# A two-layer recurrent decoder step: another rank for the token forms, other buffers for the modulation rows, one modulation vector computed earlier

## The chip, the cores and the metric

The kernel runs on one core of a Trainium2 chip. The metric is the device time of one execution in microseconds; the smaller the better.

## What is computed

Two layers over 512 prompt tokens and 8 sample rows of width 1024 (all float32). Cut to what matters here:

```python
mod = einsum('bd,de->be', silu(c), w_ada[l]) + b_ada[l]        # six vectors of 1024 per layer
sh_m, sc_m, gt_m, sh_f, sc_f, gt_f = split(mod, 6)
h = x * (1 + sc_m) + sh_m
out = mixer(h)        # layer 0: GLA and RG-LRU, layer 1: S5 and HGRN2; projections in and out
x = layer_norm(ALPHA * x + (1 + gt_m) * out, ...)
h = x * (1 + sc_f) + sh_f
x = layer_norm(ALPHA * x + (1 + gt_f) * swiglu(h, w_in, w_out), ...)   # hidden width 2816
```

Beside x, the states of the four recurrences are outputs.

## The kernel before

Columns of x are tokens: 2 halves (hf) of 256 prompt tokens and 4 samples each, 260 wide, and 8 blocks (k) of 128 features. The program runs through layer 0's mixer, the first feed-forward, layer 1's mixer (called the odd one) and the second feed-forward; a feed-forward has two parts (hb) of 11 blocks of its hidden width each. Each float32 product is made of three TensorE matmuls on parts "hi" and "lo" of both factors: `mm3` (L284, L286, L288) for a block of both halves, and its one-half form (L865 to L867) for the first units behind a LayerNorm, which start on the first half while the second half is still being normalized.

Weights come through one place, the class WS. SP loads a piece of up to 1 MB (L213) into one of three buffers named raw; ScalarE casts it to whi (L242), VectorE subtracts to get wlo (L111 is the line of every VectorE add, subtract and multiply), and TensorE reads these. The list `plan` gives the order of the pieces; `mix(main, ada)` spreads the pieces "ada" of the modulation weights among the others. One modulation vector is four ada pieces of 1 MB. Each gives 8 matmuls straight from raw (`ada_part`, L372); after the fourth, `ada_rows` copies the row out of PSUM (adasb, L377), transposes it twice (L148), and VectorE adds it into mod. The first two vectors are made at the start, column block by column block, by `ada_mm` (L361, copy L364, L366), each block just ahead of the columns of h that need it. The copies adasb lie in the pool tag t2k, six buffers that many steps share. `layer_norm` makes its columns in a ring of four buffers named h32h (L808 to L816): GpSimd or ScalarE writes h32h, ScalarE the hi part, VectorE subtracts for the lo part (L816).

A scheduler sets the order of the instructions of every engine: it goes by the order of the program, less the offset that `tc.high_priority` gives (a larger offset means earlier; HIGH is 3000). WS prepares weights at offset HIGH. SP's loads run in the order in which it issues them, and it stands when a buffer is not free.

In the odd layer, the S5 input u is turned round through DRAM: four stores Ud and one Usd (L1829, L1849), then ten loads of u (L1851 to L1853), then the matmuls at L1870. In the second feed-forward, eight products per block are replaced by seven in the manner of Strassen (`sw_unit`, L941 to L943); `t_forms` makes the sums and differences of token halves for it (t1, t2, t4, each with hi and lo part), on VectorE and ScalarE.

The change touches lines 329 to 335 (plan), 358 to 364, 375 to 377, 504 and 1020.

Of the kernel before, what the change touches and what calls it, by code (L numbers as in the profile page):

```python
# [7 lines left out]
F32 = mybir.dt.float32  # L8
# [11 lines left out]
HP = 256  # L20
# [13 lines left out]
HIGH = 3000  # L34
# [6 lines left out]
def build(tc, I, O):  # L41
    nc = tc.nc
    V, S, G, T, SY = nc.vector, nc.scalar, nc.gpsimd, nc.tensor, nc.sync
    with ExitStack() as ctx:
        def pool(n, b=1, **k):
            return ctx.enter_context(tc.tile_pool(name=n, bufs=b, **k))

        cst = pool("cst")
# [3 lines left out]
        tmp = pool("tmp", 6)  # L52
# [14 lines left out]
        def mx():  # L67
            return ps["M"].tile([128, 512], F32, tag="mx", name="mx")
# [41 lines left out]
        def tt(out, a, b, op):  # L110
            V.tensor_tensor(out=out, in0=a, in1=b, op=op)  # L111
# [38 lines left out]
        plan = []  # L150
# [144 lines left out]
        def p_ada(l, js):  # L295
            return [("ada", I["w_ada"][l], k0, 2, D * j, D, l) for j in js for k0 in range(0, 8, 2)]
# [19 lines left out]
        def mix(main, ada, first=1, per=2):  # L316
            r = list(main[:first])
            rest = main[first:]
            done = 0
            for n, c in enumerate(rest):  # L320
                want = (n + 1) * (len(ada) // per) // len(rest) * per
                r += ada[done:want]
                done = want
                r.append(c)
            return r

        FA = p_ada(0, [5]) + p_ada(1, [0])
        FB = p_ada(1, [1, 2])
        OA = p_ada(1, [3, 4, 5])
        plan.append(("lr", ev_in, 0, 8, 1536, 16))  # L330
        plan += p_cols("in", ev_in, [0])
        plan += mix(p_cols("in", ev_in, EV_COLS), p_ada(0, range(2, 4)))
        plan += mix(p_cols("out", ev_out, (0, 256)), p_ada(0, [4])[:2], 1) + p_ada(0, [4])[2:] + p_cols("out", ev_out, (512, 768))
        plan += mix(p_ffn(0, 0)[:12], FA[:4], 3) + mix(p_ffn(0, 0)[12:], FA[4:])
        plan += mix(p_ffn(0, 1)[:-4], FB, 2) + p_ffn(0, 1)[-4:]
        plan += mix(p_cols("in", od_in, OD_COLS), OA, 0, 1)
        plan.append(("glu", I["od_s5_w_glu"][0], 0, 4, 0, 512))
        plan += p_cols("out", od_out, range(0, D, 256))
# [16 lines left out]
        def vb(nm, j=0, n=1):  # L355
            return vB[:, vB_off[nm] + j:vB_off[nm] + j + n]

        def ada_mm(p, r):
            for k in range(8):
                c = k % 4  # L360
                T.matmul(p[32 * c:32 * c + 32, 0:256], condT[:, k, :], r[:, k, :],  # L361
                         start=(k < 4), stop=(k >= 4), tile_position=(0, 32 * c), skip_group_check=True)
            sb = tmp.tile([128, 256], F32, tag="t2k", name="adasb")
            S.copy(sb, p[:, 0:256])  # L364
            for b in range(2):
                T.matmul(p[:, 256 + 16 * b:256 + 16 * b + 9], sb[:, 128 * b:128 * b + 128], sel, start=True, stop=True)  # L366
            return p[:, 256:288].rearrange("p (c r) -> p c r", r=16)[:, :, 0:9]
# [5 lines left out]
                             start=(k0 + k == 0), stop=(k0 + k == 7), tile_position=(0, 32 * c), skip_group_check=True)  # L373

        def ada_rows(p, l, j):
            sb = tmp.tile([128, 256], F32, tag="t2k", name="adasb")
            S.copy(sb, p[:, 0:256])  # L377
            for b in range(2):
                transpose(p[:, 256 + 128 * b:384 + 128 * b], sb[:, 128 * b:128 * b + 128])
            tt(mod[l][:, j:j + 8, :].rearrange("p (c b) r -> p b c r", b=2),  # L380
               p[:, 256:512].rearrange("p (b c r) -> p b c r", b=2, r=32)[:, :, :, 0:9],
               bc(vA[:, 48 * l + j:48 * l + j + 8].rearrange("p (c b) -> p b c", b=2).unsqueeze(3), [128, 2, 4, 9]), ALU.add)
# [40 lines left out]
        with tc.tile_pool(name="st", bufs=1, reuse_waits="tile") as st:  # L423
# [73 lines left out]
            for f in range(8):  # L497
                px = mx()
                for q in range(4):
                    transpose(px[:, q * 128:(q + 1) * 128], xin[:, q, f * 128:(f + 1) * 128])  # L500
                S.copy(x[:, f, :, 0:HP], hv(px))
                r = raw0.pop(f)
                with tc.high_priority(offset=2 * HIGH):
                    q = ada_mm(mx(), r)
                if f + 3 < 8:
                    load0(f + 3)
                    if f in (0, 2):
                        loadx(f // 2 + 2)
                if f == 4:
                    ws.load(3)  # L510
                with tc.high_priority(offset=2 * HIGH):
                    tt(mod[0].rearrange("p (c k) r -> p c k r", k=8)[:, 0:2, f, :], q,
                       bc(vA[:, 0:48].rearrange("p (c k) -> p c k", k=8)[:, 0:2, f].unsqueeze(2), [128, 2, 9]), ALU.add)
                    ts1(sc1[:, f], mod[0][:, 8 + f, :], 1.0, ALU.add)
                    h32s.append(modulate(f, sc1, mod[0][:, 0:8, :]))
                act(x[:, f], x[:, f], AF.Copy, scale=ALPHA)
                tc.add_manual_dep(last["act"].ins, last["split"].ins.name, NOSYNC, reason="split first")
                for k in lag[f]:
                    for hf in range(2):
                        T.matmul(lrp[rows[hf], :HN], wl[:, k, :], h32s[k][:, hf], start=(k == 0),  # L520
                                 stop=(k == 7), tile_position=(0, 32 * hf), skip_group_check=True)
# [362 lines left out]
        def ffn(l, mid=None):  # L884
            with tc.tile_pool(name=f"ff{l}", bufs=1, reuse_waits="tile") as fp:
# [92 lines left out]
                for hb in range(2):  # L978
                    f0 = 11 * hb
                    fins = []  # L980
                    for d in range(0, 11, 2):
                        if l and f0 + d >= SW0:
                            break
                        nj = min(2, 11 - d)
                        fins += [(0, d, j) for j in range(nj)] + [(1, d, j) for j in range(nj)]
                    sg = {}

                    def fin_w(up, d, j):
                        return ws.get("fin", DFF * up + 128 * (f0 + d), 0, j)

                    def fin_ev(up, d, j, acc, hs=BOTH):
                        m = d + j
                        if up == 0:
                            if hs.start == 0:
                                sg[m] = t2k("sg")
                            act(sg[m][:, hs], acc, AF.Silu)
                            if hb == 0 and hs.stop == 2 and 3 <= m <= 10:
                                affine(last["act"], [m - 3])
                        else:
                            s_ = sg[m][:, hs]  # L1000
                            mul(s_, acc, s_)
                            split(ah[:, m, hs], al[:, m, hs], s_)
                            if hs.stop == 2:
                                sg.pop(m)

                    n0 = 0
                    if hb == 0:
                        n0 = 5
                        first_units([(lambda u=u: fin_w(*u), lambda acc, hs, u=u: fin_ev(*u, acc, hs)) for u in fins[:n0]], walloc)
                    for u in fins[n0:]:  # L1010
                        w = fin_w(*u)
                        acc = acc_tile()
                        mm3(acc, w, h, range(8))
                        fin_ev(*u, acc[:, :, :HN])
                        if hb == 0 and mid is not None:
                            side = side or mid(fp)
                            next(side, None)
                    if l:
                        if hb == 0:
                            with tc.high_priority(offset=200):  # L1020
                                tf[:] = t_forms()
                        pg.close()
                        with tc.tile_pool(name=f"pS{hb}", bufs=8, space=PSUM, reuse_waits="tile") as ps["S"]:
                            for f in range(max(SW0, f0), f0 + 11):
                                sw_unit(f)
                        pg.enter_context(psum(2, 4, f"g{hb}"))
                        if hb:
                            swx.close()
                    for _ in side or ():
                        pass  # L1030
                    if hb == 0:
                        gt1 = gate1(l, 5)
                    for mp in range(4 - 2 * hb):
                        accs = [acc_tile() for _ in range(2)]
                        for n, (k0, nk) in enumerate(((8, 3), (0, 8))):
                            for j in range(2):
                                w = ws.get("fout", 256 * mp, f0 + k0, j)
                                mm3(accs[j], w, a, range(k0, k0 + nk), n == 0, n == 1, koff=k0)
                        for j in range(2):
                            m = 2 * mp + j  # L1040
                            if hb == 0:
                                evac_a(m, accs[j], gt1)
                            else:
                                evac_y(m, accs[j], gt1)
# [1128 lines left out]
```

## Time and profile before

| | |
|---|---|
| time, median of 3 runs | 1405.61 us (1401.35 to 1406.16) |
| the profiled execution | 1406.39 us, span 1404.6 us, mean granted clock 0.973 |
| PE (TensorE matmuls) busy | 1321.8 us, 94% of the span, 12503 instructions |
| DVE (VectorE) busy | 865.9 us, 62% |
| ACT (ScalarE) busy | 549.4 us, 39% |
| POOL (GpSimd) busy | 187.8 us, 13% |
| moved by DMA | 185.53 MB, 132 GB/s over the span |

The first table of a kernel like this says which engine has no slack; where that engine is busy 94% of the span, the next view to read is the list of its gaps, with what ended each. The mean over the span hides that they lie at few places: the start, the recurrences, and the seams between the stages.

### The profile page before, as it was taken

Reading aid. Unit: us, or ns where it says so; the run is one execution under the profiler, and the core shown is the slowest. Engines: PE = TensorE matmul, PEld = TensorE weight load, DVE = VectorE, ACT = ScalarE, POOL = GpSimd, SP = SyncE. Lnnn points to the kernel's source line nnn. Section 1 sums busy time; section 2 is a strip of 40 time slices with the busy share of each in tenths; the row PEclk is TensorE's granted clock in tenths of the full one; section 3 lists DMA queues with packets and bytes.
Section 4 is the critical chain, followed back from the end, with each engine's and each line's share of the span. In section 5 each row is a group of like instructions: output and inputs, shape, how many; then the busy total and the mean of one; then the engine's idle time right before and its main releaser. Section 6 shows DMA issues by size and latency. Waiting matters only on the chain.

```text
span 1404.6 us, 29570 instructions
## 1 busy us (share of the span) xinstructions
PE 1321.8 (94%) x12503; PEld 1251.7 (89%) x12503; DVE 865.9 (62%) x1946; ACT 549.4 (39%) x962; POOL 187.8 (13%) x215
## 2 busy tenths in 40 slices
PE   6898999999999999999988989999897999999996
PEld 4697987989998999999978889888897999999996
DVE  4677654687998233233682586476937843788565
ACT  3554635353333222222354123344534532455431
POOL 2200010250011200000160251112600000000013
PEclk9998999999999999999999999999999999999998
DMA  9642264413346752445368636632131323332311
GB/s 270 201 149 100 73 199 148 134 48 111 131 162 216 206 174 91 150 132 180 125 226 139 213 120 198 189 110 91 61 91 30 102 84 114 105 93 73 125 61 62
DMA packets 172191, 185.53 MB, mean 132 GB/s; under 512 B 18413, under 2 KB 151915, under 8 KB 171803
## 3 DMA queue, kind: packets, MB, share of 16 engines
q1 hardware_dynamic: 166074, 166.43, 37.9%
q0 software_dynamic: 5744, 17.08, 3.7%
q8 instruction: 98, 1.61, 0.5%
q14 instruction: 35, 0.28, 0.1%
q10 hardware_dynamic: 240, 0.13, 0.0%
HBM read 167.11 MB, written 15.36 MB: 130 GB/s over the span
## 4 chain that ended last, share of the span: by engine, by line
PE 75%; DVE 10%; DMA 7%; issue 3%; ACT 2%; POOL 1%; SPq 1%; POOLq 0%; ACTq 0%; DVEq 0%
PE acc L286 15%; PE acc L284 15%; PE acc L288 15%; PE sb L941 4%; PE sb L943 3%; PE sb L942 3%; PE acc L865 3%; PE acc L867 3%; PE acc L866 3%; PE mx L372 2%; DVE wlo L111 2%; PE mx L148 2%; DMA raw<-in_w_ada_dram 2%; DVE x L111 1%; DMA raw<-in_ffn_w_out_dram 1%
## 5 line engine op out<-in xcount | busy, mean ns | idle before, releaser
L111 DVE TENSOR_TENSOR wlo<-raw,whi 128x1024 fp32r<-128x1024 f32 (+2 forms) x214 | 215.2, 1015 | 182.9 <-ACT whi L242 163.9
L242 ACT CAST whi<-raw 128x1024 fp32r<-128x1024 f32 (+2 forms) x166 | 154.2, 935 | 397.1 <-PE acc L286 269.7
L284 PE MATMUL acc<-hhi,whi 128*128 128x260 f32 x1424 | 294.4, 288 | 3.2 <-ACT hhi L79 0.9
L286 PE MATMUL acc<-hlo,whi 128*128 128x260 f32 x1424 | 293.9, 287 | 0.6 <-DVE hlo L111 0.6
L288 PE MATMUL acc<-hhi,wlo 128*128 128x260 f32 x1424 | 290.9, 286 | 0.0
L284 PEld LDWEIGHTS acc<-hhi,whi 128*128 128x128 f32 x1424 | 220.6, 190 | 15.0 <-issue 5.9
L286 PEld LDWEIGHTS acc<-hlo,whi 128*128 128x128 f32 x1424 | 221.1, 189 | 4.7 <-issue 2.7
L288 PEld LDWEIGHTS acc<-hhi,wlo 128*128 128x128 f32 x1424 | 221.2, 189 | 2.4 <-issue 1.9
L284 PE MATMUL acc<-ah,whi 128*128 128x260 f32 x576 | 117.0, 285 | 3.6 <-ACT whi L242 2.8
L286 PE MATMUL acc<-al,whi 128*128 128x260 f32 x576 | 116.1, 283 | 0.9 <-DVE al L111 0.9
L288 PE MATMUL acc<-ah,wlo 128*128 128x260 f32 x576 | 115.3, 283 | 0.0
L284 PEld LDWEIGHTS acc<-ah,whi 128*128 128x128 f32 x576 | 88.4, 188 | 7.3 <-ACT whi L242 4.3
L286 PEld LDWEIGHTS acc<-al,whi 128*128 128x128 f32 x576 | 88.6, 188 | 1.3 <-DVE al L111 1.3
L288 PEld LDWEIGHTS acc<-ah,wlo 128*128 128x128 f32 x576 | 88.5, 188 | 0.0
L111 DVE TENSOR_TENSOR smp<-acc,gt 128x8 f32<-128x8 f32 (+1 forms) x72 | 11.6, 161 | 110.9 <-PE acc L288 85.7
L865 PE MATMUL acc<-hhi,whi 128*128 128x260 f32 x208 | 60.7, 293 | 3.0 <-ACT hhi L823 2.2
L867 PE MATMUL acc<-hlo,whi 128*128 128x260 f32 x208 | 59.9, 295 | 2.0 <-DVE hlo L111 1.6
L866 PE MATMUL acc<-hhi,wlo 128*128 128x260 f32 x208 | 60.1, 291 | 0.0
L111 DVE TENSOR_TENSOR wxl<-raw,wxh 128x512 fp32r<-128x512 f32 (+1 forms) x74 | 56.3, 777 | 5.0 <-ACT wxh L160 2.9
L111 DVE TENSOR_TENSOR sg<-acc,sg 128x520 f32<-128x520 f32 (+1 forms) x32 | 19.8, 630 | 52.1 <-PE acc L288 47.6
L160 ACT CAST wxh<-raw 128x512 fp32r<-128x512 f32 x64 | 38.3, 619 | 29.0 <-PE sb L942 20.2
L372 PE MATMUL mx<-raw,condT 128*32 128x256 f32 x640 | 45.2, 391 | 2.8 <-DMA raw<-in_w_ada_dram 2.8
(640 smaller groups left out, 2856.5 us busy)
## 6 DMA issues: line engine op xcount, KB each, us to landing
raw<-in_w_ada_dram SPq DMA_DIRECT2D x40, 1024.0 KB, 6.8
raw<-in_ffn_w_in_dram SPq DMA_DIRECT2D x26, 1024.0 KB, 5.1
raw<-in_ffn_w_in_dram SPq DMA_DIRECT2D x36, 512.0 KB, 4.8
raw<-in_ffn_w_out_dram SPq DMA_DIRECT2D x16, 1024.0 KB, 5.2
raw<-in_ev_w_in_dram SPq DMA_DIRECT2D x10, 1024.0 KB, 8.3
raw<-in_od_w_in_dram SPq DMA_DIRECT2D x10, 1024.0 KB, 6.5
raw<-in_w_ada_dram SPq DMA_DIRECT2D x16, 512.0 KB, 7.5
raw<-in_ffn_w_out_dram SPq DMA_DIRECT2D x16, 384.0 KB, 3.0
```

The costliest lines, as they stand in the source:

```text
L111: V.tensor_tensor(out=out, in0=a, in1=b, op=op)
L242: S.copy(hi[:, :nk, :m], rj)
L284: T.matmul(acc[:, hf, :HN], wh[:, k - koff, :], ah(k)[:, hf, :], start=st, stop=False)
L286: T.matmul(acc[:, hf, :HN], wh[:, k - koff, :], al(k)[:, hf, :], start=False, stop=False)
L288: T.matmul(acc[:, hf, :HN], wl[:, k - koff, :], ah(k)[:, hf, :], start=False, stop=sp)
L372: T.matmul(p[32 * c:32 * c + 32, 0:256], condT[:, k0 + k, :], r[:, k, 256 * c:256 * c + 256], start=(k0 + k == 0), stop=(k0 + k == 7), til ...
L865: T.matmul(out, wh[:, k, :], ah(k)[:, hf, :], start=n == 0, stop=False)
L866: T.matmul(out, wl[:, k, :], ah(k)[:, hf, :], start=False, stop=False)
L867: T.matmul(out, wh[:, k, :], al(k)[:, hf, :], start=False, stop=n == len(ks) - 1)
L941: T.matmul(out[:, 0], w[0][:, off + k], t[0][:, k], start=st and k == 0, stop=False, skip_group_check=True)
L942: T.matmul(out[:, 0], w[1][:, off + k], t[0][:, k], start=False, stop=False, skip_group_check=True)
L943: T.matmul(out[:, 0], w[0][:, off + k], t[1][:, k], start=False, stop=k == 3, skip_group_check=True)
```

## The change

Four edits. The last vector of layer 1, the gate of its feed-forward, leaves the list of the odd layer's input projection and joins those that are computed in the second part of the first feed-forward. `ada_mm` copies into a buffer of its own in the pool of the start. `ada_rows` copies into the ring h32h. And `t_forms` gets offset HIGH instead of 200.

```diff
         FB = p_ada(1, [1, 2])
-        OA = p_ada(1, [3, 4, 5])
+        OA = p_ada(1, [3, 4])
+        LA = p_ada(1, [5])
...
-        plan += mix(p_ffn(0, 1)[:-4], FB, 2) + p_ffn(0, 1)[-4:]
+        plan += mix(p_ffn(0, 1)[:-4], FB + LA, 2) + p_ffn(0, 1)[-4:]
         plan += mix(p_cols("in", od_in, OD_COLS), OA, 0, 1)
...
-        def ada_mm(p, r):
+        def ada_mm(p, r, st):
...
-            sb = tmp.tile([128, 256], F32, tag="t2k", name="adasb")
+            sb = st.tile([128, 256], F32, tag="adasb", name="adasb")
...
         def ada_rows(p, l, j):
-            sb = tmp.tile([128, 256], F32, tag="t2k", name="adasb")
+            sb = cst.tile([128, HP], F32, tag="h32h", name="adasb", bufs=4)
...
                 with tc.high_priority(offset=2 * HIGH):
-                    q = ada_mm(mx(), r)
+                    q = ada_mm(mx(), r, st)
...
                         if hb == 0:
-                            with tc.high_priority(offset=200):
+                            with tc.high_priority(offset=HIGH):
                                 tf[:] = t_forms()
```

Lines of the changed kernel from 331 on carry a number one higher. How the change moves instructions, at three places:

DVE at the start, where the columns h of the first input are made (mod is the modulation, vB a table of small vectors, from which z, bgh, mxl, ba and el are computed for the decays); a piece of the difference:

```order
 L111 TENSOR_TENSOR hlo<-h_375,hhi 128x520
-L527 COPY vB<-mx 128x80
-L129 TENSOR_SCALAR z<-vB 128x4
 L111 TENSOR_TENSOR mod_87<-mx,vA 128x2x9
-L129 TENSOR_SCALAR bgh<-vB 128x4 x2
-L111 TENSOR_TENSOR z<-z,vB 128x4
 L129 TENSOR_SCALAR sc_105<-mod_87 128x9
-L111 TENSOR_TENSOR mxl<-vB 128x4
-L129 TENSOR_SCALAR ba<-vB 128x8
-L126 TENSOR_SCALAR er_p<-z 128x4
 L126 TENSOR_SCALAR h_405<-x,sc_105,mod_87 128x2x256
 L111 TENSOR_TENSOR h_405<-x,sc_105 128x2x4
```

The seventh column (h_405) and its modulation stand ahead of vB and z now; these rows follow behind h_405.

SP in the odd layer, from the table rot to the loads of u, before:

```order
L1856 DMA rot<-ROTd 128x2048
L1829 DMA Ud<-ut 128x512
L213 DMA raw<-in_w_ada_dram 128x2x1024
L1829 DMA Ud<-ut 128x512 x2
L213 DMA raw<-in_od_w_in_dram 128x8x256
L1829 DMA Ud<-ut 128x512
L1849 DMA Usd<-u_s 128x4x8
L1851 DMA u_8363<-Ud 16x32x64 x8
L1852 DMA u_8363<-Usd 16x32x8
```

and now:

```order
L1857 DMA rot<-ROTd 128x2048
L1830 DMA Ud<-ut 128x512
L213 DMA raw<-in_od_w_in_dram 128x8x256
L1830 DMA Ud<-ut 128x512 x2
L213 DMA raw<-in_od_w_in_dram 128x8x256
L1830 DMA Ud<-ut 128x512
L1850 DMA Usd<-u_s 128x4x8
L213 DMA raw<-in_w_ada_dram 128x2x1024
L1852 DMA u_8413<-Ud 16x32x64 x8
L1853 DMA u_8413<-Usd 16x32x8
```

A weight piece stands where a modulation piece stood, and a modulation piece has come between the store Usd and the loads of u.

POOL in the LayerNorm between the first feed-forward and the odd layer (x<-x,mu subtracts the mean of a half, four columns each; h32h are the columns), before:

```order
L785 TENSOR_TENSOR x<-x,mu 128x256 x4
L743 TENSOR_TENSOR s_7614<-s_7614,x 128x260
L812 TENSOR_SCALAR h32h<-x,gg,bb 128x256 x2
L1937 MEMSET P_9355 128x512
L812 TENSOR_SCALAR h32h<-x,gg,bb 128x256 x4
L785 TENSOR_TENSOR x<-x,mu 128x256 x4
L812 TENSOR_SCALAR h32h<-x,gg,bb 128x256 x6
```

and now:

```order
L786 TENSOR_TENSOR x<-x,mu 128x256 x4
L744 TENSOR_TENSOR s_7660<-s_7660,x 128x260
L813 TENSOR_SCALAR h32h<-x,gg,bb 128x256 x2
L1938 MEMSET P_9366 128x512
L813 TENSOR_SCALAR h32h<-x,gg,bb 128x256 x2
L786 TENSOR_TENSOR x<-x,mu 128x256 x4
L813 TENSOR_SCALAR h32h<-x,gg,bb 128x256 x8
```

Two columns of the first half have gone behind the four subtractions of the second half. On PE, 24 instead of 51 of the first units' matmuls now stand ahead of the second half's statistics there, and 16 instead of 24 modulation matmuls around their end; 130 instead of 117 matmuls of `mm3` stand ahead of the first at L1870, and 32 instead of 64 modulation matmuls behind it. From the GLU of the odd layer to the end, the rows of all five engines are the same before and after, with the engines that each waits for.

## Rows read from the trace of the kernel before

**Rows 1.** The page: busy time, 40 slices of the span, the chain by engine.

```profile
PE 1321.8 (94%) x12503; PEld 1251.7 (89%) x12503; DVE 865.9 (62%) x1946; ACT 549.4 (39%) x962; POOL 187.8 (13%) x215
...
PE   6898999999999999999988989999897999999996
...
GB/s 270 201 149 100 73 199 148 134 48 111 131 162 216 206 174 91 150 132 180 125 226 139 213 120 198 189 110 91 61 91 30 102 84 114 105 93 73 125 61 62
...
PE 75%; DVE 10%; DMA 7%; issue 3%; ACT 2%; POOL 1%; SPq 1%; POOLq 0%; ACTq 0%; DVEq 0%
```

**Rows 2.** Busy time by stretch: PE, PEld, DVE, ACT, POOL, granted clock, DMA share, GB/s.

```profile
760.00:780.00 20.00, 12.06 (x135) 11.80 (x134) 7.35 (x18) 8.57 (x13) 2.48 (x4) 0.83 1.08 139
820.00:840.00 20.00, 16.84 (x372) 15.14 (x371) 19.65 (x24) 4.37 (x8) 11.81 (x7) 0.91 0.19 58
1060.00:1080.00 20.00, 18.24 (x150) 17.82 (x149) 16.86 (x29) 9.52 (x17) 0.00 (x0) 1.00 0.18 53
1080.00:1100.00 20.00, 12.77 (x78) 12.26 (x79) 16.57 (x29) 8.29 (x18) 0.00 (x0) 0.74 0.18 54
```

**Rows 3.** Timeline of PE, 1072 to 1092: start, duration, [idle before, releaser].

```profile
1075.85 0.39 PE L941 MATMUL sb<-hhi,whi 128*128 128x260 f32 x1 [1.71 <-DVE sg L111]
...
1081.31 0.39 PE L943 MATMUL sb<-t1l,wxh 128*128 128x260 f32 x1 [1.36 <-DVE t1l L111]
...
1086.17 0.59 PE L942 MATMUL sb<-t2h,wxl 128*128 128x260 f32 x1 [3.99 <-DVE wxl L111]
...
1090.86 0.56 PE L941 MATMUL sb<-hhi,wxh 128*128 128x260 f32 x1 [1.93 <-DVE sb L111]
```

**Rows 4.** Timeline of the start, 46.5 to 53.2, all engines.

```profile
46.57 0.55 PE L366 MATMUL mx<-sel,adasb 128*128 128x9 f32 x4
...
46.94 0.97 POOL L1337 MEMSET rmask<- 128x1024 f32 x1
47.05 3.17 DVE L129 TENSOR_SCALAR z<-vB 128x4 f32<-128x4 f32 x1
...
50.62 0.54 DVE L126 TENSOR_SCALAR h<-x,sc,mod 128x512 f32<-128x512 f32 x1
...
51.23 1.22 DVE L111 TENSOR_TENSOR wlo<-raw,whi 128x1024 fp32r<-128x1024 f32 x1
...
52.58 0.62 PE L520 MATMUL mx<-h,wl 128*16 128x260 f32 x4 [2.86 <-DVE h L111]
```

**Rows 5.** Timeline of PE in the even mixer, 124 to 130.

```profile
129.35 0.86 PE L1071 MATMUL mx<-X 64*32 64x32 f32 x47 [3.92 <-issue]
```

**Rows 6.** The chain that ended last, 690 to 850: start, duration, what.

```profile
781.13 1.86 PE mx L372 x32
...
784.20 0.37 PE mx L148 x2
```

**Rows 7.** Timeline at the LayerNorm before the odd layer, PE and POOL.

```profile
709.91 0.36 PE L865 MATMUL acc<-hhi,whi 128*128 128x260 f32 x1 [0.78 <-DVE x L123]
...
711.13 0.39 PE L867 MATMUL acc<-hlo,whi 128*128 128x260 f32 x1 [0.74 <-DVE hlo L111]
...
720.17 2.99 POOL L785 TENSOR_TENSOR x<-x,mu 128x256 f32<-128x256 f32 x4 [1.50 <-ACT mu L790]
...
730.61 1.07 PE L372 MATMUL mx<-raw,condT 128*32 128x256 f32 x16 [1.72 <-DMA raw<-in_w_ada_dram]
```

**Rows 8.** Round trip of u: the chain, PE's timeline, DMA rates from 748 to 776.

```profile
751.34 8.90 DMA Ud<-ut
...
774.10 1.19 PE L1870 MATMUL mx<-u,bt 128*64 128x72 f32 x15 [7.93 <-DMA u<-Usd]
...
GB/s 205 287 380 404 392 215 48 136 214 272 274 357 272 150 120 47 25 1 0 152 156 108 83 105 82 105 82 105 82 105 83 105 83 86 116 94 164 415 427 304
```

**Rows 9.** Timeline at the HGRN2 values, PE and SP's queue.

```profile
835.49 0.90 PE L148 MATMUL mx<-ident,vt 128*128 128x128 f32 x3 [3.16 <-ACT vt L1118]
...
828.81 0.37 SPq L213 DMA_DIRECT2D raw<-in_od_w_in_dram  x1
```

## The prediction

> **What bounds the kernel.** I read the page first, then the stretches, then the idle time of TensorE place by place. The page [rows 1] shows PE busy 1321.8 of 1404.6 us (94%) and the chain that ended last running 75% over PE: whatever does not shorten PE's own work or one of its waits is worth nothing. PE's idle time sums to some 80 us, so a change that only moves work has that to win, spread over many places. The table of stretches [rows 2] shows where PE is poor: 760 to 780 us (12.06 of 20, granted clock 0.83), 820 to 840 (16.84, while DVE is busy 19.65 of 20) and 1080 to 1100 (12.77, clock 0.74). 1060 to 1080 gives the price of one projection matmul at full clock: 18.24 us for 150 of them, 0.12 us each. A value under 1 says that in part of the stretch the engine ran at 1.2 instead of 2.4 GHz, here after the gaps named below.
>
> The sum is made against the profiled execution, 1406.4 us (span 1404.6 and 1.8 around it); the median of the three runs is 1405.6, 0.8 lower.
>
> **Token forms: 0.** The gaps that this part could close are four, PE's waits for sg, t1l, wxl and sb at the first Strassen units: 1.71 + 1.36 + 3.99 + 1.93 = 9.0 us [rows 3]. But the instructions of all engines, with what they wait for, stand in the same order in both programs from the GLU of the odd layer on, the forms among them: DVE makes every form at the place where it made it. The larger rank has nothing to move. So I cost it at 0, and everything after about 915 us should repeat.
>
> **Start: -1.5.** TensorE waits 2.86 us for h of the seventh column [rows 4]. On DVE a 4-element z starts at 47.05 and lasts 3.17 us, while GpSimd fills first rmask (from 46.94) and then P; h comes behind it at 50.62, a wlo of 1.22 us stands between its parts, and PE has it at 52.58. The vector's own buffer lets the scheduler put mod, sc and h ahead of vB and z. Two bounds: if h gets through before the fills, the whole 2.86 is saved; if it meets them, h itself waits until z's end, 50.2, and then needs what it needs now less the 1.22 us wlo: PE has it at about 51.3, and 1.3 us are saved. mod needs the matmuls of 46.57, so h would start at about 47.2, just behind the first fill; I take -1.5, near the second bound. Zero is the other end of the range (z's stall moves to an operation that PE waits for next).
> The Trainium skill bears on this: SBUF: State Buffer, "Who interferes with whom", says that VectorE's second port pair is GpSimd's, held for a whole instruction, and that the one which issues second fully blocks. The trace agrees with 3.17 us for four elements; by that rule alone h would be blocked too, and the sum would have -1.3 here.
>
> **Even mixer: -1.** The small matmuls of the GLA levels are less bunched; in the old order PE stands for 3.92 us behind them with no releaser [rows 5]. It can vanish (-3.9), or come twice (+3.9). Nothing in the trace says what it is, so I take a quarter of it.
>
> **First feed-forward, second half: +2.2.** Four more 1 MB pieces pass PE there: 32 matmuls, 1.86 us where the chain shows such a vector, and two transposes at 0.37 us [rows 6]. PE is 9 tenths and more in these slices [rows 1], so all of it counts. Four more loads pass SP; the slices of this half, the 16th to the 20th, moved 91 to 180 GB/s [rows 1], where the first slice moved 270, so they have room. If the loads do hold up a weight, one such wait as the 1.72 us of [rows 7] is the price, once or twice: +2.2 to +5.6.
>
> **LayerNorm behind it: -2.** PE's waits here are 0.78 and 0.74 for the first column, and 1.72 for the modulation's weights [rows 7], 3.2 together. Now 24 instead of 51 first-unit matmuls stand ahead of the second half's statistics (27 x 0.12 us = 3.2 us earlier, of which the sums on DVE allow about two), and 16 instead of 24 modulation matmuls behind them, so the third piece is not waited for. What speaks against it: the vector's buffer now comes out of the ring of four that the columns use, and GpSimd does two columns of the first half only after the four subtractions of the second, 2.99 us in [rows 7]. Bounds -3.2 and +3.0. I take -2, since PE has 27 more matmuls to do when those two columns come late.
>
> **The round trip of u: -0.6.** This is the largest single gap: 7.93 us, until the last u load has landed at 774.10 [rows 8]. 13 more matmuls of the input projection (at 0.12 us, 1.6 us) now stand ahead of it; they would fill that much of the gap. But SP's queue has a new element between the store Usd and the eight loads of u: 1 MB of modulation weights. The last store of Ud is issued at 751.34 and has landed 8.90 us later, at 760.24; the rates in the same group show that the transfers run dry from about 758.5 to 761 and that the peak is over 415 GB/s, at which 1 MB takes 2.5 us. So most of it passes while SP waits for the stores anyway. I take +1 for it. Bounds: nothing, and 11 us, if its 1 MB shares the pipe with the u loads at the 94 GB/s or so that these have. The wait of SP in front of it, for PE to have used the piece before, is met: those matmuls stand ahead of the last 130 of the projection, some 15 us before PE needs u.
> The Trainium skill would have it dearer: DMA: Bandwidth & Descriptors, "Queues, rings and completion order", says that each DMA engine takes its descriptors in ring order, so a load in front delays what is behind it by its whole transfer. No row here shows a load of that size directly in front of u; by the rule alone the term would be +2.5 and the sum 1.5 worse.
>
> **Odd layer after it: -1.9 and -1.5.** 32 modulation matmuls and two transposes are gone from the stretch behind the S5 input (2.2 us by the same rows); bounds -2.2 and 0, if DVE sets the pace there. DVE does between 812 and 842: PE waits 3.16 us for vt, which stands on ACT behind the cast of a weight whose load was issued only at 828.81 [rows 9], after a wlo. The mod, gg and bb operations leave this stretch on DVE, one scan leaves it too, and the load's place in the queue is one piece earlier. Half of the 3.16 is my value; bounds -3.16 and 0.
>
> **Sum:** -1.5 - 1 + 2.2 - 2 - 0.6 - 1.9 - 1.5 = -6.3, so 1406.4 - 6.3 = 1400.1 us. Against the median that is 5.5 us or 0.4%, inside the 0.5% (7.0 us) that a measurement of this kernel can tell from no change.
>
> **Rivals.**
> All gaps close: start -2.9, mixer -3.9, LayerNorm -3.2, u -1.6, projection -2.2, vt -3.2, against +2.2: -14.8, 1391.6, with most of it 1394. For it: each wait has its releaser in the rows. Against: six independent gains. Chance 0.22.
> The forms do move the end (that DVE's rows are alike does not hold on the chip): another -9.0, 1391. Against it stand the identical orders. 0.04.
> Given back: every microsecond won before u is waited for at u, since the stores and the 94 GB/s loads set that end, and PE's extra vector in the feed-forward is paid in full. Start and mixer give -2.5, the feed-forward +2.2, the waits up to u nothing, and of the 3.4 behind it a sixth stays: -0.9, 1405.5, nothing that can be measured. 0.18.
> Slower: the new load before the u loads. If it is issued late (its buffer is PE's to free) or shares the pipe with them, u lands up to 11 us later, of which 1.6 is covered: -6.3 - 1 + 11 = +3.7, 1410.1; with another 3 to 6 us in which SP stands before it, 1413 to 1416. It decides from the point at which u lands some 7 us later, counted from the last store's issue, than the 22.8 us of [rows 8] (751.34 to 774.10). For it: SP waits in order. Against: the dry time in the transfers. 0.14.
> Forecast, 0.42.
>
> **How the numbers follow.** A third of the forecast's cases (0.14), all-gaps (0.22) and forms (0.04) are faster by over 0.5%, below 1398.6: 0.40. The rest of the forecast (0.28), given back (0.18) and the milder part of the slower case (0.04): 0.50. Its harder part, above 1412.6: 0.10. The range 1393 to 1410 leaves out the forms, the lowest part of all-gaps and most of the slower case, together under 0.2.
>
> **What would show it.** After the change: the DVE row of z still long, but h before it and PE's 2.86 us under 1.6; 32 modulation matmuls more between 530 and 690 us; the LayerNorm's stretch without the wait for the modulation's load; the time from the last Ud store's issue to the first S5 matmul within 2 us of 22.8; the wait for vt halved; and from the GLU on every gap as before, the four of [rows 3] among them. The forecast is wrong if those four shrink, or if u lands over 4 us later relative to its stores.

## The result, and the profile after

| | before | after |
|---|---|---|
| time, median of 7 runs each | 1401.35 us (1396.06 to 1406.16) | 1391.95 us (1391.06 to 1395.02) |
| ratio, 95% interval | | 0.9937 (0.9913 to 0.9962) |
| profiled execution, its span | 1406.39 us, 1404.6 us | 1392.64 us, 1390.9 us |

The kernel became faster by 0.6%, 8.8 us (5.3 to 12.2) by the ratio; the two medians lie 9.4 us apart. The page says first that PE's work stayed the same and its idle time shrank: 1320.2 busy of 1390.9 us leaves 70.7 us, where it was 82.8 [rows 1]. Some of that is scatter: a second profile of the kernel before, in the first experiment below, has 79.1.

```profile
PE 1320.2 (95%) x12503; PEld 1252.0 (90%) x12503; DVE 866.3 (62%) x1946; ACT 551.6 (40%) x962; POOL 191.4 (14%) x215
```

The four waits at the first Strassen units, from the timeline of PE after the change; they answer to [rows 3]:

```profile
1060.29 0.39 PE L942 MATMUL sb<-hhi,whi 128*128 128x260 f32 x1 [1.71 <-DVE sg L111]
1065.75 0.39 PE L944 MATMUL sb<-t1l,wxh 128*128 128x260 f32 x1 [1.36 <-DVE t1l L111]
1070.61 0.59 PE L943 MATMUL sb<-t2h,wxl 128*128 128x260 f32 x1 [3.99 <-DVE wxl L111]
1075.30 0.56 PE L942 MATMUL sb<-hhi,wxh 128*128 128x260 f32 x1 [1.93 <-DVE sb L111]
```

To the hundredth they are the same four numbers. The stretch of 1060 to 1080 is now as poor as 1080 to 1100 was [rows 2]:

```profile
1060.00:1080.00 20.00, 12.42 (x70) 11.73 (x71) 17.64 (x30) 6.88 (x15) 0.00 (x0) 0.68 0.18 52
```

At the start, all engines' timeline shows what became of h [rows 4]:

```profile
45.10 4.35 DVE L126 TENSOR_SCALAR h<-x,sc,mod 128x512 f32<-128x512 f32 x1
...
45.91 0.97 POOL L1338 MEMSET rmask<- 128x1024 f32 x1
...
46.80 1.83 POOL L1459 MEMSET P<- 128x2048 f32 x1
...
48.55 0.54 POOL L1461 MEMSET P<- 128x512 f32 x1
...
49.70 0.17 DVE L129 TENSOR_SCALAR z<-vB 128x4 f32<-128x4 f32 x1
...
49.80 0.62 PE L521 MATMUL mx<-h,wl 128*16 128x260 f32 x4 [1.40 <-DVE h L111]
...
52.17 0.50 PE L286 MATMUL acc<-hlo,whi 128*128 128x260 f32 x2 [0.97 <-DVE hlo L111]
```

z takes 0.17 us now and h takes 4.35: the stall stayed and found another instruction. PE's wait fell from 2.86 to 1.40 us, since z, the small operations and a wlo no longer stand between. But PE waits again 2.4 us later, 0.97 us for the lo part hlo of the same column, where it had no wait before.

At u, SP's queue and PE's timeline [rows 8]:

```profile
742.24 0.64 SPq L1830 DMA_DIRECT2D Ud<-ut  x1
742.97 0.66 SPq L1850 DMA_DIRECT2D Usd<-u_s  x1
744.15 1.88 SPq L213 DMA_DIRECT2D raw<-in_w_ada_dram  x1
...
765.10 3.17 PE L1871 MATMUL mx<-u,bt 128*64 128x72 f32 x48 [5.21 <-DMA u<-Ud]
```

From the last store of Ud to the first S5 matmul it is 22.86 us, 22.8 before; the new load of 1 MB stands in the queue, and the gap is 2.7 us shorter than the 7.93 of [rows 8].

### The profile page after: what moved, and what is told of

Read it like the earlier page. It is cut to its first block, busy times and chain, and to the rows that moved or that the text cites. A ratio compares the mean times of both kernels' runs of the same rounds, so it can differ in the third digit from the quotient of the medians.

```text
span 1390.9 us, 29577 instructions
## 1 busy us (share of the span) xinstructions
PE 1320.2 (95%) x12503; PEld 1252.0 (90%) x12503; DVE 866.3 (62%) x1946; ACT 551.6 (40%) x962; POOL 191.4 (14%) x215
## 5 line engine op out<-in xcount | busy, mean ns | idle before, releaser
L111 DVE TENSOR_TENSOR wlo<-raw,whi 128x1024 fp32r<-128x1024 f32 (+2 forms) x214 | 212.2, 1001 | 164.3 <-ACT whi L242 146.3
L942 PE MATMUL sb<-hhi,wxh 128*128 128x260 f32 x128 | 38.1, 298 | 7.0 <-DVE sb L111 7.0
```

What stands on the lines that cost most here:

```text
L942: T.matmul(out[:, 0], w[0][:, off + k], t[0][:, k], start=st and k == 0, stop=False, skip_group_check=True)
```

## The experiments

**One part at a time.** Each kernel is the one before with one edit of the change, and each ratio here and below is taken against runs of the kernel before that were made beside it. Four kernels were measured beside one another:

```diff
-                            with tc.high_priority(offset=200):
+                            with tc.high_priority(offset=HIGH):
                                 tf[:] = t_forms()
```

> Only the rank of the token forms is changed (200 to HIGH). Theory by place (the change is won at the start, in the even mixer and in the odd layer, the forms move nothing): all rows stand in the same order as before, so ratio 1.000 within its interval (0.997 to 1.003), and the four gaps of PE at the first Strassen units are 1.71, 1.36, 3.99 and 1.93 us again. Rival (the rank moves the end): 9 us less, ratio 0.9935, and the gap of 3.99 us under 1. This kernel is also a second sample of before's profile: if its gaps in the even mixer (3.92) and at u (7.9) differ by more than 1 us from before's, that much of the difference between the two profiles is scatter.

Measured 1.0008 (0.9994 to 1.0021). Every row of every engine stands where it stood before, so this is the kernel before in all but name, and its profile is a second sample of it: 1395.2 us of span, 9.4 less than the first. The gap in the mixer is 4.41 (3.92), that at u 7.68 (7.93), so those differ by under 1 us; the 9.4 lie elsewhere, in waits and in the clock. One such place is the LayerNorm: between 715 and 740 us nearly the same instructions ran at a granted clock of 0.92 in the first profile and 1.00 here. The runs of the program before spread over 1394 to 1406 us, and the profile shown ahead of the prediction was from their slow end.

> Only ada_mm's copy has a buffer of its own. Theory by place: the start and the even mixer are won here, the wait for h falls from 2.86 to 1.4 us and the clock of 50 to 75 us rises from 0.93 to 1.00; 3 us at 75 us, 3 to 6 us by 150 us, and nothing more behind the even mixer: ratio 0.996 to 0.998. Rival (the odd layer's move is the whole gain): ratio 1.000.

```diff
-            sb = tmp.tile([128, 256], F32, tag="t2k", name="adasb")
+            sb = st.tile([128, 256], F32, tag="adasb", name="adasb")
```

(the first of two such lines, in `ada_mm`.) Measured 1.0000 (0.9984 to 1.0015): the rival's number. The wait for h fell to 1.40 us as expected, but the granted clock of 50 to 75 us was 0.86, and what the even mixer won was lost again further on (below, at "Even mixer").

> Only ada_rows copies into the ring h32h. The start is as before (2.86 us wait for h). Theory by place: the copies no longer compete with the steps that use t2k, which moves only the groups of modulation matmuls between 170 and 500 us: 0 to -3 us, ratio 0.998 to 1.000. Rival (the ring costs the LayerNorm its columns): the waits at the LayerNorms grow by 1 to 3 us each, ratio 1.001 to 1.004.

```diff
-            sb = tmp.tile([128, 256], F32, tag="t2k", name="adasb")
+            sb = cst.tile([128, HP], F32, tag="h32h", name="adasb", bufs=4)
```

(the second line, in `ada_rows`.) Measured 0.9965 (0.9948 to 0.9982), 4.9 us, more than either expectation: over half of the whole, from the edit that looked smallest.

> Only the last modulation vector is moved into the first feed-forward. Theory by place: 64 more modulation matmuls of the trace pass between 530 and 690 us and cost 4 us there; the odd layer up to its GLU gives 8 to 10 us back (4 for the same matmuls, 2 to 3 at u, 2 to 4 at vt and the S5 output); net -4 to -6 us, ratio 0.996 to 0.997. Rival (a gain before u is waited for at u): net +1 to -1, ratio 1.000.

```diff
-        OA = p_ada(1, [3, 4, 5])
+        OA = p_ada(1, [3, 4])
+        LA = p_ada(1, [5])
...
-        plan += mix(p_ffn(0, 1)[:-4], FB, 2) + p_ffn(0, 1)[-4:]
+        plan += mix(p_ffn(0, 1)[:-4], FB + LA, 2) + p_ffn(0, 1)[-4:]
```

Measured 0.9987 (0.9973 to 1.0002), less than the theory's 0.996 to 0.997; it can't be told from no change.

**All but the moved vector.** Both buffers and the rank:

> The change without its moved vector: both buffers and the rank, the plan of before. If the parts add up (rows buffer -4.9 us, ada_mm's buffer 0, moved vector -1.8, rank 0): -5 us, ratio 0.9965. If the two buffers together open what neither opens alone (the trace has 8 us by the first LayerNorm in the change, 1.8 and 4.6 with one buffer each): -7 to -8 us, ratio 0.9945 to 0.995, and the moved vector is then worth about nothing. If the moved vector is the greater part: ratio above 0.998.

Measured 0.9945 (0.9925 to 0.9965). The whole change has 0.9937 (0.9913 to 0.9962): the vector's move adds nothing that these runs can tell. Whether the two buffers together are more than one and one (7.7 us against 4.9 and 0) can't be told either, the intervals overlap.

**Where it lies.** With PE's timelines of all these kernels one can time the stages between points that every kernel passes: the first statistics matmul of the three LayerNorms (A behind the even layer, B behind the first feed-forward, C behind the odd layer), the first S5 matmul and the first matmul of the GLU. In us, each one profile:

| kernel | to A | A to B | B to S5 | S5 to GLU | GLU to C |
|---|---|---|---|---|---|
| before | 276.0 | 423.3 | 74.9 | 136.2 | 75.3 |
| before again (rank alone) | 274.9 | 421.2 | 72.5 | 136.1 | 71.9 |
| ada_mm's buffer | 273.2 | 421.5 | 73.4 | 137.7 | 74.4 |
| ada_rows' buffer | 270.4 | 422.2 | 72.2 | 132.1 | 74.0 |
| moved vector | 275.7 | 427.2 | 71.0 | 132.7 | 73.5 |
| both buffers | 268.1 | 422.2 | 72.2 | 132.9 | 72.6 |
| the change | 266.8 | 428.1 | 70.2 | 132.9 | 72.3 |

The last column has the same instructions in all seven (with the moved vector, PE and DVE take a few of them in another order) and differs by 3.4 us: that is the scatter of one profile, and the measure for the others. The profile is also one execution of its kernel, up to 5 us off the median of its runs. Read so, and against the second profile of before, three things stand out. To A, the buffers give 1.7 and 4.5 us one by one and 6.8 together; the 1.7 lies inside the scatter. A to B, the moved vector costs 4 to 7 us. S5 to GLU falls by 3.4 to 4 us with ada_rows' buffer alone, by as much with the moved vector alone, and by no more with both.

That last sum looks like one wait that either part takes away, but the rows of that stretch show two different things. In this order: before again, ada_rows' buffer, the moved vector, the change, and a later kernel (the one of "The stall at the start") whose instructions stand here in the order of the change:

```profile
768.70:904.79 136.09, 132.40 (x1962) 122.32 (x1963) 85.66 (x164) 35.08 (x70) 32.66 (x30) 0.97 0.58 183
764.78:896.85 132.07, 131.02 (x1960) 121.61 (x1961) 85.56 (x167) 35.38 (x70) 31.70 (x30) 0.98 0.61 189
773.88:906.59 132.71, 129.03 (x1885) 121.59 (x1885) 83.16 (x162) 34.78 (x69) 32.90 (x30) 0.95 0.50 151
765.10:897.96 132.86, 129.30 (x1885) 122.66 (x1886) 83.89 (x162) 34.51 (x68) 33.52 (x30) 0.94 0.50 152
760.07:887.45 127.38, 123.91 (x1885) 117.11 (x1886) 83.88 (x162) 34.51 (x68) 33.53 (x30) 0.99 0.52 160
```

(The first three numbers are the stretch, its length and PE's busy time with its matmuls; the granted clock is the third from the end.) The buffer takes PE's idle time from 3.7 to 1.1 us, with nearly the same work. The moved vector takes work away: 77 of PE's matmuls are gone, and its busy time falls by 3.4 us; the wait for vt is gone too, but the idle time stays at 3.7, in waits at other places, and the granted clock is 0.95. In the change PE waits 1.80 and 1.76 us some 56 and 77 us behind the first S5 matmul, and the clock is 0.85 and 0.81 in the two stretches of 10 us from 70 us on. Where the clock stayed at 0.99, the same instructions took 5.5 us less. So the moved vector can win something of its own here, but only in that one profile; in the other four that have it, the change's among them, the clock is 0.94 to 0.95 and takes it back.

**What the second ring did in the odd layer.** The copies of the modulation rows shared the six buffers t2k with much else, R of the S5 scans among it (L1956). To test whether that held the scan back, only the three vectors made in the odd layer were given the ring h32h, in the kernel before:

```diff
         def ada_rows(p, l, j):
-            sb = tmp.tile([128, 256], F32, tag="t2k", name="adasb")
+            if l and j >= 24:
+                sb = cst.tile([128, HP], F32, tag="h32h", name="adasb", bufs=4)
+            else:
+                sb = tmp.tile([128, 256], F32, tag="t2k", name="adasb")
```

> The kernel before, with only the copies of the odd layer's vectors (gate of the mixer, shift and scale behind it: the vectors 3 to 5 of layer 1) in the ring h32h; plan, start and even layer as before. DVE's order differs in two places: the first S5 scan (its table R lies in t2k) stands some ten rows earlier, and one addition into mod. Theory (the ring t2k held the scan back, and the scan held back the subtraction that frees a weight buffer): the weight load in the HGRN2 projection is issued 8 to 9 us earlier, the wait of 2.9 to 3.2 us for vt goes, and 3 to 4.5 us by 890 us: ratio 0.997 to 0.998. Rival (the moved vector or the LayerNorm brings that gain): the wait for vt stays, ratio 1.000.

Measured 0.9960 (0.9940 to 0.9981), 5.6 us (2.7 to 8.4): as much as ada_rows' whole buffer, within the intervals. The wait for vt, first in the kernel before (its second profile; DVE, SP's queue, ACT and PE):

```profile
807.80 2.33 DVE L1961 TENSOR_TENSOR_SCAN vr<-R,vr 128x512 f32<-128x512 f32 x2
...
821.01 2.24 DVE L111 TENSOR_TENSOR wlo<-raw,whi 128x1024 fp32r<-128x1024 f32 x1
...
823.28 0.37 SPq L213 DMA_DIRECT2D raw<-in_od_w_in_dram  x1
...
828.13 1.04 ACT L242 CAST whi<-raw 128x1024 fp32r<-128x1024 f32 x1 [7.83 <-DMA raw<-in_od_w_in_dram]
...
829.71 0.66 PE L148 MATMUL mx<-ident,vt 128*128 128x128 f32 x4 [2.85 <-ACT vt L1118]
```

and with the odd layer's copies out of t2k:

```profile
793.35 2.33 DVE L1964 TENSOR_TENSOR_SCAN vr<-R,vr 128x512 f32<-128x512 f32 x2
...
818.12 1.23 DVE L111 TENSOR_TENSOR wlo<-raw,whi 128x1024 fp32r<-128x1024 f32 x1 [0.37 <-ACT whi L242]
...
819.37 0.37 SPq L213 DMA_DIRECT2D raw<-in_od_w_in_dram  x1
...
824.65 1.05 ACT L242 CAST whi<-raw 128x1024 fp32r<-128x1024 f32 x1 [2.49 <-PE acc L286]
...
828.54 0.60 PE L148 MATMUL mx<-ident,vt 128*128 128x128 f32 x4
```

Read from below: PE's wait is gone, because the cast waits for PE's own product and no longer for a transfer; the transfer was issued 3.9 us earlier, at the end of the wlo that reads its buffer; and that wlo is earlier because the first pair of scans runs at 793 us, in a stretch where DVE had room, and not at 808. The load was expected 8 to 9 us earlier and came 3.9 (5.1, counted from the first S5 matmul). S5 to GLU is 132.6 us.

**The forms.** DVE makes them through temporary sums q, and q lies in the same ring t2k, behind the sg of the feed-forward. A rank cannot pass a buffer. In this experiment q gets memory of its own, the part of ah and al that is not written yet (further lines of the edit make that part of single tiles); the rest is the whole change:

```diff
+                def qt(nm):
+                    return fp.tile([128, 2, HN], F32, tag=f"z{free.pop(0)}", name=nm)
...
-                        q1, q2, q3 = t2k("q1"), t2k("q2"), t2k("q3")
+                        q1, q2, q3 = qt("q1"), qt("q2"), qt("q3")
```

> The change, and the sums q of the token forms in memory of their own (space of ah and al that is not yet used) in place of the pool t2k. Theory (it is the buffer that holds the forms behind the last sg, no rank can move them): the forms stand 40 to 60 rows earlier on DVE, beside the LayerNorm; of the four gaps at the first Strassen units (1.71, 1.36, 3.99, 1.93 us) at least 6 us go, and the clock there rises from 0.68: 7 to 10 us less than the change, ratio to before 0.986 to 0.989. Rival (DVE is full there anyway, the forms only push out the LayerNorm's lo parts and the weights): less than 2 us, ratio 0.992 to 0.994.

Measured 0.9904 (0.9882 to 0.9927), so 4.6 us less than the change, between the two expectations; the two intervals overlap a little, and the next run shows such a gain clear of its interval. The first lo part is made at 1011 us, where it was made at 1065 (t1l, DVE's timeline), and of the four waits one of 0.75 us is left. The 20 us from the first Strassen matmul on, which is at 1067.02 here and at 1060.29 in the change, to compare with the row of the change above:

```profile
1011.65 0.68 DVE L111 TENSOR_TENSOR t1l<-q,t1h 128x520 fp32r<-128x520 f32 x1
```

```profile
1067.02:1087.02 20.00, 19.24 (x159) 18.82 (x158) 16.18 (x30) 11.57 (x25) 0.00 (x0) 1.00 0.36 106
```

PE does 159 matmuls there in place of 70, at the full granted clock in place of 0.68. From the first Strassen matmul to PE's last it is 11.3 us less (314.1 against 325.4), but from C to the first 3.6 us more (93.6 against 90.0): the sums now stand among the LayerNorm's lo parts on DVE, and a wait for sg behind it is 3.28 us where it was 2.73.

> The kernel before (rank 200, all else as it was), with the same memory for q alone. Theory of the buffer: the same gain as in the run before it has over the change, 7 to 10 us with the old rank: ratio 0.993 to 0.995. If the rank matters once the buffer is free: under half of that gain.

Measured 0.9962 (0.9947 to 0.9977), 5.3 us (3.2 to 7.4) with the old rank: less than the 7 to 10 expected, and clear of zero. So it is the buffer; no effect of the rank can be seen with it or without it.

**The stall at the start.**

```diff
+                with tc.high_priority(offset=2 * HIGH):
                     G.memset(rmask, 1.0)
...
+                with tc.high_priority(offset=2 * HIGH):
                     G.memset(P, 0.0)
                     G.memset(P32, 0.0)
```

> The change, and GpSimd's fills of rmask and P issued before its wait for the transposed table, at about 10 us, in place of 46 to 49 us. If a VectorE operation with two ports stands still while GpSimd writes: h of the seventh column takes 0.5 to 1.6 us (the DMA issues on GpSimd before it remain) in place of 4.35, PE's wait of 1.40 us goes: -1 to -2 us against the change, ratio 0.992. If the fills have nothing to do with it, h takes 4.35 again.

Measured 0.9919 (0.9900 to 0.9939). The fills did not go to 10 us: their row, too, shows a wait for PE's transposes (L148), probably for memory that these still use, and they start at 43.12 in place of 45.91. That is enough:

```profile
46.62 1.13 DVE L126 TENSOR_SCALAR h<-x,sc,mod 128x512 f32<-128x512 f32 x1
```

h takes 1.13 us in place of 4.35, with one short fill of 0.97 us still beside it, and PE's wait for it is gone. The point A is passed at 262.3 us, 4.5 earlier than in the change: more than the 1.40 us of the wait. It is no chance of one profile, as the two kernels below that have the same fills pass A at 261.9 us; where the rest comes from stays open. The time alone does not show the gain: 2.5 us lie between the two ratios, and their intervals overlap.

**Together.** Both fills and forms on top of the change, without and with the moved vector:

> Both buffers of the change, the old plan, the forms' sums in memory of their own and the early fills. If the parts add (buffers -7.7 us, forms -4.6, fills -2.5): ratio 0.9895. If the waits that go turn up elsewhere: 0.991 to 0.993.

> The same with the moved vector, so all of the change. Theory (the move costs PE 4 to 5 us in the first feed-forward and gives the same back): equal to the run before it within 0.3%, ratio 0.9885 to 0.9905. If the move is worth what it was costed at in the prediction (-3 to -4 us), 0.987.

Measured 0.9872 (0.9845 to 0.9899), 1380.44 us, and 0.9852 (0.9823 to 0.9880), 1380.17 us in the median of six runs each. Both beat the change, by some 10 us. The second lies below both of its expectations. The parts at least add: 14.8 and 15.9 us were their sums, 17.9 (14.1 to 21.7) and 20.7 (16.8 to 24.8) are measured. With or without the moved vector is again the same within the intervals.

## Why the prediction was right and wrong

The direction was right and the gain was forecast as 6.3 us, where 8.8 (5.3 to 12.2) were measured. The time lay 1 us below the range; a change of under 0.5% had a chance of 0.50 and a faster kernel 0.40, where 0.6% (0.4 to 0.9) were measured. Of the 8.2 us between the forecast of 1400.1 and the median of 1391.95, 5.1 come from the base of the sum and 3.1 from its terms, which missed by more and offset one another. Step by step:

**"The sum is made against the profiled execution, 1406.4 us"; the median of three is 0.8 lower.** This is the step that failed and put the time outside the range. Those runs were the slow end of a scatter that three runs did not show: with four more the median of before is 1401.35 us, and beside the experiments it was 1399.56 to 1399.72. From 1401.35 the same sum gives 1395.1, and the range, moved down as far, is 1388 to 1405, with 1391.95 inside.

**Token forms: 0.** Right, to the hundredth of a microsecond and with the reason half right: the forms' order was unmoved, as read, and what held it was the ring that q lies in, which the prediction did not look for. That all rows from the GLU on stand as before holds in the traces only from C on: in the 22 us behind the first GLU matmul PE takes the GLU's matmuls and the sample rows' in a slightly different order, and two rows of DVE change places before C. From C to the end it is 419.0 us before and 420.6 after.

**Start: -1.5.** Right at the wait it names: by the second bound h waits through the fills itself, and the wait fell by 1.46. That it is worth 1.5 is not shown: 0.97 us come back in the wait for hlo. The buffer alone, with the same wait of 1.40, has 600 matmuls behind it at 87.9 us, where it is 87.2 in before's second profile and 85.7 in the change; the granted clock of 50 to 75 us was 0.86, 0.93 and 1.00 in these three. By the rule of the Trainium skill (SBUF: State Buffer, "Who interferes with whom": of two instructions that want the shared ports the one which issues second fully blocks) the prediction had 1.3. The trace agrees that h is held, for 4.35 us, but not in what decides it: h's row begins at 45.10, 0.81 us ahead of the first fill, and it is held through three fills, not one instruction.

**Even mixer: -1.** Too small, and the term with the largest miss. To A the change is 8.1 us ahead of before's second profile (9.1 of the first), where the start and this term foresaw 2.5. [rows 5] was the only gap of the even layer that the prediction costed. That gap, 4.41 us in the second profile, is 2.84 now, and a wait for modulation weights at 237 us is gone:

```profile
238.51 1.07 PE L372 MATMUL mx<-raw,condT 128*32 128x256 f32 x16 [1.45 <-DMA raw<-in_w_ada_dram]
```

(the kernel before, second profile, PE). Which buffer wins changes on the way. After 2200 of PE's 2801 matmuls up to A it is 196.7 us in before's second profile, 192.8 with ada_mm's buffer alone, 194.8 with ada_rows' alone and 191.5 in the change. So up to there ada_mm's buffer gives more, 3.9 us, in the mixer. Alone it loses 2 of them again before A, in two waits that the kernels with ada_rows' buffer do not have, and the granted clock is 0.66 in 230 to 240 us:

```profile
231.43 0.75 PE L284 MATMUL acc<-hhi,whi 128*128 128x260 f32 x4 [2.18 <-ACT hhi L385]
...
233.11 0.80 PE L286 MATMUL acc<-hlo,whi 128*128 128x260 f32 x2 [0.94 <-DVE hlo L111]
```

(the kernel with ada_mm's buffer alone, PE). Behind that place ada_rows' buffer wins 2.7 us more. So the one wins in the mixer, the other behind it, and together they keep both; why the term was 5.6 us short is shown so far, and what in the mixer's order is worth 4 us stays open.

**First feed-forward: +2.2.** The mechanism is right and the size under half. The order's 32 matmuls for a vector are 64 in the profile, which has two records for each of these, so the row of 1.86 us for 32 in [rows 6] was half a vector. PE's busy time of this line in 525 to 695 us, before and after:

```profile
525.00:695.00 170.00, 7.94 (x128) 3.65 (x128) 1.00 0.42 140
```

```profile
525.00:695.00 170.00, 12.02 (x192) 5.42 (x192) 1.00 0.47 159
```

4.1 us; and A to B is 6.1 us longer in the mean of the five profiles with the moved vector than in the eight without it, more than the top of the term's range, 5.6. The two us beyond the matmuls stay open. The same mistake halves the "-1.9" behind u. ada_rows' buffer has a wait here that no term foresaw: 2.78 us for al at 429 us, which is 0.89 before, as DVE makes S5 constants ahead of it; A to B is no longer with that buffer alone, though.

**LayerNorm: -2, u: -0.6.** Together 2.6 forecast; B to S5 is 1.5 us shorter with the moved vector alone and 2.4 in the change. The wait of 1.72 for the modulation's weights is gone, as foreseen. The price of the load before u can be read from all the profiles: from Ud's last store to the first S5 matmul 20.7 to 22.8 us in the eight without it, 22.1 to 24.1 in the five with it, 1.4 more in the mean, near the +1 taken. The Trainium skill (DMA: Bandwidth & Descriptors, "Queues, rings and completion order") states the ring order alone; that the load then delays u by its whole transfer, an estimate of 2.5 us from [rows 8], was the prediction's own step, and 1.1 us more than measured. That the dry time before the u loads takes the difference fits, but was not tested.

**Odd layer after it: -1.9 and -1.5.** The sum is right by luck: S5 to GLU is 3.2 us shorter in the change. The wait for vt is gone whole, but it was put down to the vector's move and needs only the buffer; and the work of the vector is gone, 4.1 us of it and not 1.9. Both together would be 7 us, and the waits at other places and the lower clock, for which the prediction had no term, took over half. With some 6 us more in the first feed-forward, 2 to 3 less up to S5 and next to nothing behind it that the buffer does not win as well, the moved vector, costed at -3.8 in sum, gave nothing that could be measured beside the buffers.

So the sum of the terms, -6.3, came near the 8.8 with errors that offset: 5.6 us too little won to A, some 4 too little paid in the first feed-forward.

Of the rivals, "all gaps close" came nearest in time (1391.6 to 1394), by the base alone: it was to win 14.8 us from six independent gaps, and these waits did not all close. "Slower" did not happen: the load before u cost 1.4 us and not up to 11.

## What to carry to other kernels

A rank orders only what is free to run: before raising one, look up which buffers the instruction takes its memory from, and who holds them. A ring shared by unlike users ties their orders together at a distance; an edit that takes one user out of it can be worth more at another user's place than at its own. A stage from which work is taken can give the time back through its waits and the granted clock, so read both there. And three runs do not show a spread of 12 us: make the sum as a difference, and put the range around the median of more of them, or widen it by the scatter.

## What the runs showed of the hardware that was not expected

The same program has profiles of 1404.6 and 1395.2 us of span. The difference sits in a few places, among them stretches with nearly the same instructions at another granted clock (0.92 and 1.00 at 715 to 740 us). Between the first S5 matmul and the GLU, 1885 PE instructions in one and the same order took 132.9 us at a granted clock of 0.94 and 127.4 at 0.99. A VectorE instruction of 0.55 us, h, took 4.35 us beside GpSimd's fills and 1.13 us when they were issued 2.8 us earlier. DMA issues of GpSimd did not hold it in that second kernel: at 50.75 us an h beside one of them took 0.55 us.
